# A mixture-of-experts product on one core: the last P4 pair unsplit, P3 begun with a pair

## The chip, the core and the metric

The kernel runs on one core of one Trainium2 chip. The metric is the device time of one execution in microseconds (us). In the text TensorE (PE) multiplies matrices, VectorE (DVE) and ScalarE (ACT) work on tiles and empty TensorE's accumulators, GpSimd (POOL) and SyncE (SP) mostly issue DMA transfers; ScalarE issues some too. Every engine takes its instructions in program order.

## What is computed

Each token is multiplied by all eight experts' matrices, and the results are added with softmax weights:

```python
def reference(x, router_logits, expert_weights):      # (16, 512, 512), (16, 512, 8), (8, 512, 2048)
    probs = softmax(router_logits, axis=-1)
    output = np.zeros((16, 512, 2048), np.float32)
    for e in range(8):
        output += probs[:, :, e:e+1] * np.matmul(x, expert_weights[e])
    return output
```

Put differently: with the tokens in one row of 8192 and the scaled inputs p_e * x of all experts side by side, the output is one product of an 8192 x 4096 and a 4096 x 2048 matrix.

## The kernel before

**Three levels of fast products.** The kernel forms that product with seven multiplications in place of eight, on three levels. On the outer level the tokens are cut into 16 blocks q of two halves of 256, the experts into two groups of four and the output columns into two halves; the seven outer products are called P1, P2, P5, P6, P7, P4 and P3 and run in about this order, each for all sixteen q. On the middle level an outer product of one q (class `Product`, line 566) has seven steps in the order of `STEPS` (1, 5, 6, 2, 7, 3, 4; line 353). Each step is eight matmuls of 128 x 128 by 128 x 512, for which it needs a left operand (128 tokens) and a right one, called a weight here, one for each step. On the innermost level steps 1 and 5 of a *pair* of products can be done together by seven smaller products each (`by_thirds`, line 781): 56 matmuls of half width in place of 32 of full width. A stage in which that is done is called split here.

**Stages.** `add` (line 672) puts one or two products into a stage; stages run one after another (`run`, line 849). In a pair the steps alternate: step 1 of the first product, step 1 of the second, and so on. Work beside the products is hung on a stage and a slot (`at`, line 669): slots count the steps of the stage, 0 to 13 in a pair and 0 to 6 in a single; in a split stage slots 0 to 3 are spread over the split part. k4 is the first stage of P4 and k3 the first of P3; P4 has eight pairs, k4 to k3-1, all of them split. P3 has a single (3,0) in stage k3, seven pairs in k3+1 to k3+7, and a single (3,15) in the last stage, `end` = k3+8; k3+2 to k3+7 are split. (3,0) stands for product P3 of q = 0.

**Left operands.** A `Left` (line 445) is made by VectorE out of two loads, xT and pT, in two halves (`queue_make`), with a difference d (`queue_s2`) and an interpolation (`queue_i`, z<-z,d). For P3 a third load is subtracted from each half, the left operand of P6 that was put by in DRAM (`ZBlock`, line 494, w<-z in the profile). It takes a buffer of tag w. The operands of a stage are made in the stage before it (`queue_lefts`), their loads begin two stages before (`start_loads`), unless a hook places them (`load_z`, line 1152).

**Weights.** P3's seven weights come from DRAM with one 1 MB load each, issued by ScalarE (`fetch_w`, line 162, w<-wd in the profile): three were stored as they are (tag b22), four are sums that were made in parts during P4 (`by_parts`, line 1071). `turnover` (line 1128) hangs the seven fetches, in the order of STEPS, on slots counted on from a stage, 14 to a pair. For split stages the weights of steps 1 and 5 are cut up into sums of their own (`third_sums`, line 178, called by `make_third`, line 1159), one more buffer of tag w each.

**The w buffers.** The pool `wpool` has 15 buffers of 1 MB with tag w. They hold, in P4 and P3: the seven weights of the outer product, two third sums, in each split stage a room tile for the sums of the left operands, in each split stage of P4 a keep tile (`keep_in_w`, line 1210) in which results wait that go to DRAM at the end of the stage (out_dram<-keep), the tile of `by_parts`, the seven weights of the next outer product as they come, and the ZBlocks of P3. A new tile gets the buffer that the program gave up first; the instruction that first writes it waits until the last user of the old tile is done, and what is behind it on its engine waits too.

**Order on VectorE.** A list of tasks is filled by hooks and emptied by `slack` (line 384): after each step it puts as many tasks into VectorE's program as a count of its time leaves room for. `post` (line 582) puts in what empties the accumulators: on P4, which adds to a base that was loaded from DRAM (h<-out_dram), six of seven posts are VectorE's and one (step 2, line 616) is ScalarE's; on P3 two are VectorE's and five ScalarE's. The base of the corner (1,0) is loaded by hook into a half of the keep tile (keep<-out_dram, lines 929 to 933), those of the others into h tiles. The results go out through GpSimd, where they are added to what is in DRAM.

**The end.** The last product, (3,15), adds to a base of its own, whose four parts are fetched in the stage before it (lines 1173 to 1177).

Of the kernel before, what the change touches and what calls it, by code (L numbers as in the profile page):

```python
# [31 lines left out]
def kernel(  # L32
# [84 lines left out]
    def sp(o, i):  # L117
        note(nc.sync.dma_start(out=o, in_=i))

    def pool(o, i, **how):  # L120
        note(nc.gpsimd.dma_start(out=o, in_=i, **how))  # L121
# [40 lines left out]
    def fetch_w(what, kn):  # L162
        t = new_w()
        note(nc.scalar.dma_start(out=t, in_=stored[what, kn]))  # L164
        return t
# [12 lines left out]
    def third_sums(w):  # L178

        t = new_w().rearrange("p (s c) (h n) -> p s c h n", s=2, h=2)  # L180
        t = {5: t[:, 0, :, 0], 6: t[:, 0, :, 1], 7: t[:, 1, :, 0], 4: t[:, 1, :, 1]}
        b = w.rearrange("p (k c) (h n) -> p k c h n", k=2, h=2)
        tt(t[5], b[:, 0, :, 1], b[:, 0, :, 0], SUB)
        tt(t[6], b[:, 1, :, 1], t[5], SUB)
        tt(t[7], b[:, 1, :, 1], b[:, 0, :, 1], SUB)
        tt(t[4], b[:, 1, :, 0], t[6], SUB)
        return {**t, 1: b[:, 0, :, 0], 2: b[:, 1, :, 0], 3: b[:, 1, :, 1]}
# [186 lines left out]
    def need(task):  # L374
        if task is not None and not task.done:
            flush(task)
            clock["pe"] = max(clock["pe"], clock["dve"])

    def later(cost, make, first=False):
        t = Task(cost, make)  # L380
        (queue.appendleft if first else queue.append)(t)
        return t
# [246 lines left out]
    def out_rows(q, odd, cols, tn):  # L629
        t, n = tn  # L630
        return out_f[ds((2 * q + odd) * HQ + t * HP, HP), ds(cols * NH + n * NB, NB)]

    def to_out(q, odd, cols, **how):
        return lambda tn, o: pool(out_rows(q, odd, cols, tn), o, **how)
# [22 lines left out]
    def base_of(q):  # L657
        if q % 2:
            return WideBase(out_f[ds(2 * q * HQ, HQ), ds(NH, NH)]
                            .rearrange("(t p) (n m) -> p t n m", t=2, n=2))  # L660
        return Base(lambda tn: out_rows(q, 0, 1, tn))

    INNER = ((0, 0), (1, 1), (0, 1), (1, 0))


    stages = []
    hooks, late, wait_for = {}, {}, {}

    def at(stage, slot, make):
        hooks.setdefault((stage, slot), []).append(make)  # L670

    def add(*products):
        stages.append(products)
        return len(stages) - 1
# [11 lines left out]
    def left_of(r, q, fresh=True):  # L686
        a, b = 2 * q, 2 * q + 1
        if r == 1:
            pt = PBlock(a, P1, xp1[q - 2][1] if q in (2, 3) else None)
            if q in (2, 3):  # L690
                xs[a] = XBlock(a, xp1[q - 2][0])
            return Left(xblock(a), pt), [xblock(a), pt]
        if r in (2, 4):
            h, pt = (a, PBlock(a, P2)) if r == 2 else (b, PBlock(b, P2))
            return Left(xblock(h), pt), [xblock(h), pt]
        if r == 5:
            pt = PBlock(b, PQ)
            return Left(xblock(b), pt), [xblock(b), pt]
        if r == 6:
            pt = PBlock(a, P1)  # L700
            return Left(xblock(a), pt, of=lefts[5, q]), [xblock(a), pt]
        h = a if r == 3 else b
        pt = PBlock(h, P2)
        if r == 7 and q >= 14:
            return Left(xblock(h), pt, kept=lefts[6, q]), [xblock(h), pt]
        kept_z = ZBlock(q)
        return Left(xblock(h), pt, kept=kept_z), [xblock(h), pt, kept_z]

    def kept_rows(q):
        return lambda tn: kept[q][tn[1], ds(tn[0] * HP, HP), :]  # L710

    def product(r, q, **how):
        left, loads = left_of(r, q)
        lefts[r, q] = left
        p = None
        if r == 1:
            def sink(tn, o):
                pool(kept_rows(q)(tn), o)
            p = Product(right[1], left, sink)
        elif r == 2:  # L720
            if q >= QK:
                base = products[1, q].o.__getitem__
            else:
                base = bases[2, q] = Base(kept_rows(q))
            p = Product(right[2], left, to_out(q, 0, 0), base)
        elif r == 5:
            bases[6, q] = m1 = Base(kept_rows(q))
            m1.task = {}

            p = Product(right[5], left, to_out(q, 1, 0))  # L730
        elif r == 6:
            m1 = bases[6, q]

            def base(tn):
                need(m1.task[tn])
                return m1.t[tn]
            p = Product(right[6], left, to_out(q, 0, 1), base)
        elif r == 7:
            base = bases[7, q] = base_of(q) if q < 14 else products[6, q].o.__getitem__
            p = Product(right[7], left, to_out(q, 1, 1), base)  # L740
        elif r == 4:
            base = bases[4, q] = Base(lambda tn: out_rows(q, 1, 1, tn))
            p = Product(right[4], left, to_out(q, 1, 0, accum_op=ADD), base)
        else:
            p = Product(right[3], left, to_out(q, 0, 1, accum_op=ADD), **how)
        p.loads = loads
        products[r, q] = p
        return p
# [30 lines left out]
    thirds = {}  # L779
# [91 lines left out]
    def fetch_at(stage, slot, base, *tns):  # L871
        for tn in tns:
            at(stage, slot, lambda tn=tn: base.fetch(tn))
# [8 lines left out]
    for i in range(0, QK + 1, 2):  # L882
        k = add(product(2, rest[i]), product(2, rest[i + 1]))
# [14 lines left out]
            ks.setdefault(r, add(product(r, q), product(r, q + 1)))  # L898
    k7, k4 = ks[7], ks[4]
    xs.clear()  # L900
    k3 = add(product(3, 0))
    for q in range(1, 15, 2):
        add(product(3, q), product(3, q + 1))
    end = add(product(3, 15))

    def claim(of, tn):
# [7 lines left out]
    for q in range(16):  # L914
        k = k5 + 1 + q
# [6 lines left out]
    def base_at(stage, slot, r, q, *tn):  # L922
        at(stage, slot, lambda: bases[r, q].fetch(*tn))
    for q in range(0, 14, 2):
        k = k7 + 1 + q // 2
# [3 lines left out]
    for q in range(16):  # L929
        k = k4 + q // 2  # L930
        for slot, tn in zip((6, 8, 10), INNER):
            base_at(k - 1, slot, 4, q, tn)
        base_at(k, 4, 4, q, INNER[3], lambda k=k: thirds[k].kept.pop())


    def wedge(kn, e):
# [122 lines left out]
    def slots_after(stage, slot, n):  # L1059
        slot += n  # L1060
        while slot >= 7 * len(stages[stage]):
            slot -= 7 * len(stages[stage])
            stage += 1
        return stage, slot
# [63 lines left out]
    def turnover(stage, slots, r, raw):  # L1128

        right[r].w = {}  # L1130

        def fetch(p):
            if p in RAW:
                right[r].w[p] = fetch_w(raw, RAW[p])
            else:
                right[r].w[p] = fetch_w((r, p), (0, 0))
        for slot, p in zip(slots, STEPS):
            at(*slots_after(stage, slot, 0), lambda p=p: fetch(p))
    turnover(k6 - 1, range(2, 15, 2), 7, "t3")
    turnover(k4 - 1, range(0, 13, 2), 4, "t4")  # L1140
    turnover(k3 - 2, (4, 12, 18, 19, 20, 21, 24), 3, "b22")

    for q in range(16):
        z_dram[q] = dram.tile([P, 2 * K8, HQ], f16, name=f"z_{q}")
# [3 lines left out]
        k, half_way = k5 + 1 + q, 7 * len(stages[k5 + q]) * 9 // 14  # L1148
# [3 lines left out]
    def load_z(stage, slot, r, q):  # L1152
        load = products[r, q].loads[-1]
        load.by_hook = True
        at(stage, slot, load.begin)
# [3 lines left out]
    def make_third(stage, slot, r, p):  # L1159
        def make():  # L1160
            third_of[r][p] = third_sums(right[r].w[p])
        at(stage, slot, lambda: third_made[r].append(later(2.76, make)))
# [1 line left out]
    make_third(k4 - 1, 7, 4, 1)  # L1164
    make_third(k4 - 1, 9, 4, 5)
    load_z(k3 - 2, 8, 3, 0)
    load_z(k3 - 1, 11, 3, 1)
    load_z(k3 - 1, 12, 3, 2)
    make_third(k3 - 1, 8, 3, 1)
    make_third(k3 - 1, 9, 3, 5)  # L1170


    finish = products[3, 15]
    finish.base = Base(lambda tn: out_rows(15, 0, 1, tn))
    finish.sink = lambda tn, o: sp(out_rows(15, 0, 1, tn), o)
    for slot, tn in zip((6, 8, 10, 12), INNER):
        fetch_at(end - 1, slot, finish.base, tn)
    finish.steps = (1, 5, 6, 3, 7, "2a", 4, "2b")
    cols = {"2a": ds(0, NB // 2), "2b": ds(NB // 2, NB // 2)}
# [30 lines left out]
    def keep_in_w():  # L1210
        t = wpool.tile([P, 4, NB], f32, name="keep", tag="w")
        return [t[:, i] for i in range(4)]
    for r, first, to, keep in ((4, k4, k3, keep_in_w), (3, k3 + 2, end, None)):
        for stage in range(first, to):
            thirds[stage] = Thirds(*(p.left for p in stages[stage]), third_of[r], new_w, keep, third_made[r])
    need_first = [right[1].task[p] for p in (6, 7, 4)]
# [41 lines left out]
```

## Time and profile before

| | |
|---|---|
| three runs, median (lowest to highest) | 1377.53 us (1374.09 to 1378.62) |
| profiled execution, its time | 1377.51 us |
| its span, first to last instruction | 1375.8 us |
| granted TensorE clock, mean | 0.994 |
| matmuls | 6798 |
| DMA | 388.43 MB, 282 GB/s on the mean |
| HBM | 241.21 MB read, 173.21 MB written |

The page of a profile lists, for each engine, busy time, share of the span and number of instructions; its other views used here are the list of waits (who waited for what: total us, times, longest us), the timeline (start us, duration us, engine, line, operation, out<-in, count, and in brackets the idle time before with what ended it), the chain of waits (the work that ended last, followed back; start us, duration us, what), the groups of instructions (busy us, mean ns of one, idle time before), the DMA issues (count, KB of each, median us from issue to landing) and windows (for a stretch of time: its length, each engine's busy us and number of instructions, TensorE's clock, DMA share, GB/s). A queue such as ACTq or SPq is the part of the engine that issues; a DMA on it is shown with the time that issuing took. DMA lines with GB/s cut a stretch into 40 equal slices. An engine's idle time matters only where TensorE then waits for it.

### The profile page before, as it was taken

To read this page: it belongs to the slowest core of one execution; us is meant where nothing else is said; L and a number is where in the kernel's file an instruction comes from. 1 tells how busy PE (TensorE), PEld (TensorE's weight loads), DVE (VectorE), ACT (ScalarE), POOL (GpSimd) and SP (SyncE) were. 2 spreads that over 40 slices of the span, in tenths; PEclk is the share of its full clock that TensorE was granted. 3 is DMA by queue.
4 is the path that set the end of the run, shared out by engine and by line. 5 is a ranking of instruction groups with operands and counts; after the bars stand their busy time and mean duration, and the time that the engine had idled before them with its cause. 6 is when DMAs were issued, how large, how long until landed. Compare 5 with 4: busy or idle time off the path is not lost.

```text
span 1375.8 us, 18714 instructions
## 1 busy us (share of the span) xinstructions
PE 1360.0 (99%) x6798; PEld 663.1 (48%) x6798; DVE 1120.3 (81%) x1386; ACT 228.1 (17%) x453; POOL 410.9 (30%) x652
## 2 busy tenths in 40 slices
PE   9999999999999999999999999999999999799998
PEld 4555444444444444444444444444555555256554
DVE  7877767579789888887978888988888889678884
ACT  3232111100011111111111100000111111133331
POOL 3223233331222343323332122222143423133231
PEclk9999999999999999999999999999999999799999
DMA  9998999999899999999999999998999999999976
GB/s 184 224 246 234 212 260 249 254 288 387 249 289 295 337 343 314 306 280 292 340 266 297 392 383 392 360 355 292 335 224 276 264 294 304 305 280 237 218 107 127
DMA packets 199229, 388.43 MB, mean 282 GB/s; under 512 B 53728, under 2 KB 87776, under 8 KB 191584
## 3 DMA queue, kind: packets, MB, share of 16 engines
q0 software_dynamic: 88688, 185.12, 55.4%
q1 hardware_dynamic: 106416, 173.68, 39.6%
q10 hardware_dynamic: 4032, 28.44, 5.3%
q8 instruction: 53, 0.87, 0.2%
q14 instruction: 40, 0.33, 0.1%
HBM read 241.21 MB, written 173.21 MB: 301 GB/s over the span
## 4 chain that ended last, share of the span: by engine, by line
PE 94%; DMA 4%; issue 1%; POOL 1%; ACTq 0%; ACT 0%; POOLq 0%
PE ps L130 71%; PE pt L130 23%; DMA w<-wd 2%; DMA out_dram<-keep 1%; DMA w<-in_expert_weights_dram 1%; POOL out_dram L121 0%; ACTq L164 0%; POOL w L121 0%; ACT h L616 0%; ACT h L1202 0%; POOL ident L225 0%; POOLq L121 0%; ACTq L616 0%; POOLq L225 0%; POOLq L1242 0%
## 5 line engine op out<-in xcount | busy, mean ns | idle before, releaser
L130 PE MATMUL ps<-w,z 128*128 128x512 f16 (+1 forms) x3760 | 823.6, 376 | 7.2 <-DMA w<-wd 7.2
L130 PEld LDWEIGHTS <-z 128*128 128x128 f16 x5280 | 517.6, 98 | 595.9 <-issue 14.8
L121 POOL DMA_DIRECT2D out_dram<-h x336 | 217.6, 664 | 681.7 <-ACT h L616 312.9
L130 PE MATMUL pt<-w,z 128*128 128x512 f16 (+1 forms) x1520 | 324.7, 361 | 2.4 <-DMA w<-wd 2.2
L107 DVE TENSOR_TENSOR h<-ps,h 128x512 f32<-128x512 f32 x253 | 171.6, 687 | 126.3 <-PE ps L130 114.1
L107 DVE TENSOR_TENSOR z<-xT,pT 128x2048 f16<-128x2048 f16 x220 | 266.3, 1217 | 3.9 <-DMA xT<-xs 2.8
L130 PE MATMUL ps<-w,d 128*128 128x512 f16 x880 | 199.2, 379 | 0.0
L130 PEld LDWEIGHTS <-d 128*128 128x128 f16 x880 | 86.1, 98 | 100.2
L107 DVE TENSOR_TENSOR z<-z,d 128x2048 f16<-128x2048 f16 x110 | 132.2, 1217 | 0.0
L107 DVE TENSOR_TENSOR w<-w 128x1024 f16<-128x1024 f16 (+2 forms) x116 | 116.3, 1016 | 2.4 <-PE ps L130 1.0
L603 ACT COPY h<-ps 128x512 f32<-128x512 f32 x90 | 52.8, 587 | 376.4 <-PE ps L130 366.6
L107 DVE TENSOR_TENSOR h<-pt,h 128x512 f32<-128x512 f32 x111 | 76.1, 687 | 42.0 <-PE pt L130 36.8
L616 ACT COPY h<-ps 128x512 f32<-128x512 f32 x57 | 33.4, 587 | 363.9 <-PE ps L130 337.2
L107 DVE TENSOR_TENSOR d<-z 128x1024 f16<-128x1024 f16 x110 | 74.5, 684 | 0.8
L107 DVE TENSOR_TENSOR z<-z,w 128x2048 f16<-128x2048 f16 x60 | 73.5, 1225 | 2.0
L107 DVE TENSOR_TENSOR ps<-ps,h 128x512 f32<-128x512 f32 (+1 forms) x77 | 48.3, 629 | 20.4 <-PE ps L130 15.9
L121 POOL DMA_DIRECT2D wd<-w x86 | 47.3, 550 | 53.9 <-DVE w L107 17.8
L121 POOL DMA_DIRECT2D w<-in_expert_weights_dram x65 | 49.0, 791 | 38.7 <-DMA wd<-w 28.2
L130 PEld LDWEIGHTS <-w 128*128 128x128 f16 x528 | 48.7, 98 | 8.1 <-DMA w<-in_x_dram 1.6
L121 POOL DMA_DIRECT2D kept<-h x56 | 30.8, 550 | 67.2 <-ACT h L603 35.1
L599 ACT COPY h<-ps 128x512 f32<-128x512 f32 x63 | 35.4, 600 | 74.9 <-PE ps L130 72.0
L107 DVE TENSOR_TENSOR h<-h 128x512 f32<-128x512 f32 (+2 forms) x69 | 45.2, 675 | 0.1
(81 smaller groups left out, 455.3 us busy)
## 6 DMA issues: line engine op xcount, KB each, us to landing
out_dram<-h POOLq DMA_DIRECT2D x336, 256.0 KB, 7.8
w<-z SPq DMA_DIRECT2D x30, 1024.0 KB, 12.6
pT<-p_dram SPq DMA_DIRECT2D x108, 256.0 KB, 9.6
w<-wd ACTq DMA_DIRECT2D x27, 1024.0 KB, 10.2
h<-kept SPq DMA_DIRECT2D x100, 256.0 KB, 7.2
h<-out_dram SPq DMA_DIRECT2D x80, 256.0 KB, 13.9
wd<-w POOLq DMA_DIRECT2D x72, 256.0 KB, 8.5
xT<-x SPq DMA_DIRECT2D x71, 256.0 KB, 10.3
```

What stands on the lines that cost most here:

```text
L107: dve(nc.vector.tensor_tensor(out=o, in0=a, in1=b, op=op))
L121: note(nc.gpsimd.dma_start(out=o, in_=i, **how))
L130: note(nc.tensor.matmul(ps, z, w, start=start, stop=stop, skip_group_check=True))
L599: act(nc.scalar.copy(o[tn], q if p == 5 else x))
L603: act(nc.scalar.copy(o[TN[p]], b if p == 2 else x))
L616: act(nc.scalar.copy(o[tn], b))
```

## The change

The order of P3's products and what hangs on it:

- the last P4 pair, stage k3-1, is no longer split, has no keep tile and no room tile, and its two (1,0) bases go into h tiles at slot 3;
- P3 consists of seven pairs, k3 to k3+6, then the single (3,14) in k3+7, then the single (3,15) as before. Split are k3+1 to k3+6;
- P3's weights 1, 5, 6, 2, 7, 3, 4 are fetched in k3-3 at slots 4 and 12, in k3-2 at slots 6 and 10, and in k3-1 at slots 2, 4 and 6. Before, they were fetched in k3-2 at slots 4 and 12 and in k3-1 at slots 4, 5, 6, 7 and 10;
- the ZBlocks of (3,0) and (3,1) come in k3-2 at slots 8 and 12, those of (3,2) and (3,3) at the first two slots of k3; before, that of (3,0) came in k3-2 at slot 8, those of (3,1) and (3,2) in k3-1 at slots 11 and 12;
- the third sums of P3's weights are queued at the start of k3 and no longer in k3-1;
- the bases of (3,15) are fetched at slots 1 to 4 of the stage before it, now a single, in place of slots 6, 8, 10 and 12 of a pair.

```diff
     k7, k4 = ks[7], ks[4]
     xs.clear()
-    k3 = add(product(3, 0))
-    for q in range(1, 15, 2):
+    k3 = len(stages)
+    for q in range(0, 14, 2):
         add(product(3, q), product(3, q + 1))
+    add(product(3, 14))
     end = add(product(3, 15))
...
             base_at(k - 1, slot, 4, q, tn)
-        base_at(k, 4, 4, q, INNER[3], lambda k=k: thirds[k].kept.pop())
+        if k < k3 - 1:
+            base_at(k, 4, 4, q, INNER[3], lambda k=k: thirds[k].kept.pop())
+        else:
+            base_at(k, 3, 4, q, INNER[3])
...
-    turnover(k3 - 2, (4, 12, 18, 19, 20, 21, 24), 3, "b22")
+    turnover(k3 - 3, (4, 12, 20, 24, 30, 32, 34), 3, "b22")
...
     load_z(k3 - 2, 8, 3, 0)
-    load_z(k3 - 1, 11, 3, 1)
-    load_z(k3 - 1, 12, 3, 2)
-    make_third(k3 - 1, 8, 3, 1)
-    make_third(k3 - 1, 9, 3, 5)
+    load_z(k3 - 2, 12, 3, 1)
+    load_z(k3, 0, 3, 2)
+    load_z(k3, 1, 3, 3)
+    make_third(k3, 0, 3, 1)
+    make_third(k3, 0, 3, 5)
...
-    for slot, tn in zip((6, 8, 10, 12), INNER):
+    for slot, tn in zip((1, 2, 3, 4), INNER):
         fetch_at(end - 1, slot, finish.base, tn)
...
-    for r, first, to, keep in ((4, k4, k3, keep_in_w), (3, k3 + 2, end, None)):
+    for r, first, to, keep in ((4, k4, k3 - 1, keep_in_w), (3, k3 + 1, end - 1, None)):
         for stage in range(first, to):
             thirds[stage] = Thirds(*(p.left for p in stages[stage]), third_of[r], new_w, keep, third_made[r])
```

## The prediction

> **What bounds the kernel now.** I read the first part of the page, then the list of waits, then the timeline of TensorE around the only place where it waits for long. The profiled execution took 1377.51 us, of which 1375.8 us are the span; the median of the three runs shown is 1377.53 us, so the sum below, made against the profiled execution, stands for the median too.
>
> ```profile
> PE 1360.0 (99%) x6798; PEld 663.1 (48%) x6798; DVE 1120.3 (81%) x1386; ACT 228.1 (17%) x453; POOL 410.9 (30%) x652
> PE ps L130 <- DMA w<-wd: 7.2, 3, 4.6
> PE pt L130 <- DMA w<-wd: 2.2, 1, 2.2
> ```
>
> TensorE sets the time. All that it waits for after the start is 9.4 us in four waits for weights (w<-wd), and the timeline of TensorE puts them side by side, in the single product (3,0) with which P3 begins (stage k3):
>
> ```profile
> 1169.39 1.89 PE L130 MATMUL pt<-w,z 128*128 128x512 f16 x8
> ...
> 1174.24 1.90 PE L130 MATMUL ps<-w,z 128*128 128x512 f16 x8 [1.23 <-DMA w<-wd]
> 1180.75 3.57 PE L130 MATMUL ps<-w,z 128*128 128x512 f16 x8 [4.62 <-DMA w<-wd]
> 1186.48 3.57 PE L130 MATMUL pt<-w,z 128*128 128x512 f16 x8 [2.16 <-DMA w<-wd]
> 1191.37 7.54 PE L130 MATMUL ps<-w,z 128*128 128x512 f16 x24 [1.32 <-DMA w<-wd]
> 1198.75 3.62 PE L130 MATMUL pt<-w,z 128*128 128x512 f16 x16
> ...
> 1219.47 1.04 PE L130 MATMUL pt<-w,z 128*128 128x256 f16 x8
> ...
> 1242.85 1.04 PE L130 MATMUL pt<-w,z 128*128 128x256 f16 x8
> ```
>
> A step is eight matmuls. From 1198.75 to 1219.47 twelve unhindered steps pass: 1.727 us each. From 1169.39 (step 5 of the single) to 1198.75 (step 5 of the next pair) there are eight steps, 13.8 us, but 29.36 us go by: 15.5 us are lost. That is more than the 9.4 us of waiting, since eight matmuls take 3.57 us instead of 1.89 after the longest wait. The chain of waits, the timeline of ScalarE and its queue, and that of GpSimd tell why the weights are late:
>
> ```profile
> 1145.47 14.28 DMA out_dram<-keep
> ...
> 1162.57 28.75 DMA w<-wd
> ```
>
> ```profile
> 1134.12 0.59 ACT L616 COPY h<-ps 128x512 f32<-128x512 f32 x1 [1.14 <-PE ps L130]
> 1139.56 0.33 ACTq L164 DMA_DIRECT2D w<-wd  x1
> ...
> 1159.81 1.63 ACTq L164 DMA_DIRECT2D w<-wd  x3
> 1161.56 0.59 ACT L616 COPY h<-ps 128x512 f32<-128x512 f32 x1 [10.61 <-DVE z L107]
> ```
>
> ```profile
> 1122.16 0.86 POOL L121 DMA_DIRECT2D out_dram<-keep  x1 [0.46 <-DVE keep L107]
> ```
>
> Five of P3's seven weights are asked for in the last P4 stage, k3-1. The first of them waits until the keep tile of stage k3-2 has been written out (1145.47 + 14.28 = 1159.75), and then five fetches go out within 3 us; the last lands at 1191.33 (1162.57 + 28.75). The fifteen buffers of tag w are handed on in the order in which the program gives them up: the third tiles and the room tile of k3-1, idle once the split part ends, 23.38 - 10 x 1.727 = 6.1 us into the stage, go to later requests. The second fetch, too, goes out at 1139.56, 4.9 us after ScalarE's copy has ended: it takes the keep tile of k3-3, whose last write was issued at 1122.16.
>
> **The change, part by part.**
>
> *One split less.* A split stage lasts 1242.85 - 1219.47 = 23.38 us, an unsplit pair 14 x 1.727 = 24.18 us. P4 has seven split stages for eight; P3 keeps six. Cost +0.80 us, on the path.
>
> *Weights earlier.* The seven fetches move from k3-2 (two) and k3-1 (five) to k3-3 (two), k3-2 (two) and k3-1 (three). The unsplit k3-1 needs no room tile and no keep tile, and the two third tiles of P4 come free one stage earlier, at about 1127. Handing the buffers on in order: weight 1 takes the keep tile of k3-5, weight 5 that of k3-4, weight 6 the tile of the last part sums, weight 2 a third tile, weight 7 the other one. All of these are free before they are asked for or soon after, so weights 1, 5, 6, 2 and 7 land tens of us before k3 begins at 1144.28 + 24.18 = 1168.46 (the single began one step before 1169.39, at 1167.66, and k3-1 and k3-2 each 23.38 us earlier, at 1144.28 and 1120.90). Weights 3 and 4 get the first weight of P4 and the keep tile of k3-2, free at 1159.75; in a pair each step lasts 3.45 us, so weight 3 is needed at 1168.5 + 5 x 3.45 = 1185.7. ScalarE may stand until 1160 with the two copies of step 2 (due at 1156.4 and 1158) behind it. The same happens now without cost: the copy of k3-1 runs at 1161.56 after 10.61 us, and TensorE does not wait. Gain: the whole 15.5 us; 1377.5 - 15.5 + 0.8 = 1362.8 us if nothing else is late.
>
> *What is late next: the left operand of (3,0).* Its load (call it z0, w<-z) keeps its slot in k3-2, but the buffer that it gets is now the keep tile of k3-3, which weight 5 had. That is not free before about 1139.5, as the fetch above shows, where z0 went out at 1129.77 before:
>
> ```profile
> 1129.77 0.33 SPq L118 DMA_DIRECT2D w<-z  x1
> 1131.78 4.49 SPq L118 DMA_DIRECT2D h<-out_dram  x2
> w<-z SPq DMA_DIRECT2D x1, 1024.0 KB, 20.7
> w<-z SPq DMA_DIRECT2D x2, 1024.0 KB, 11.4
> w<-z SPq DMA_DIRECT2D x3, 1024.0 KB, 13.9
> 1144.48 0.69 DVE L107 TENSOR_TENSOR keep<-ps,keep 128x512 f32<-128x512 f32 x1 [0.44 <-PE ps L130]
> 1157.66 1.23 DVE L107 TENSOR_TENSOR z<-z,w 128x2048 f16<-128x2048 f16 x1
> L107 DVE TENSOR_TENSOR z<-z,d 128x2048 f16<-128x2048 f16 x110 | 132.2, 1217 | 0.0
> L107 DVE TENSOR_TENSOR d<-z 128x1024 f16<-128x1024 f16 x110 | 74.5, 684 | 0.8
> ```
>
> Behind it on SP stand two bases h of k3-1, then the load z1 of (3,1), xT and pT. z0 lands 11.4 to 20.7 us after its issue (the DMA issues of the three stages k3-2, k3-1, k3), so between 1150.9 and 1160.2. VectorE comes to it sooner than the 1157.66 of before: without the third sums and the sums for a split k3-1 its queue is empty at the end of k3-2, and after its last addition at 1145.2 stand one interpolation (1.22), the first post (0.69), the other one (1.22), the second post (0.69) and the product of the operand (1.22): it waits for z0 from 1150.2. Behind that wait stand the posts of steps 5 and 6. The second post of step 6 comes 1.22 + 2 x 0.69 + 0.69 + 0.69 + 2.45 + 0.69 = 7.1 us after z0 has landed, and TensorE needs it for its tenth step at 1144.28 + 9 x 1.727 = 1159.8. So what z0 lands later than 1152.7 is lost. Ends: nothing, and 7.5 us, to which slow matmuls add up to 2 x 1.68 (3.57 - 1.89). From the middle duration, 13.9, and 1.5 us more for the keep tile, whose write now runs beside two fetches more, z0 lands at 1154.9: I take 2.5 us with the base loads behind it. Whether the clock falls in so short a gap decides another 1.7 us; after 1.23 us in the rows above it did not (1.90), after 4.62 it did, so I take none.
>
> The Trainium skill, TensorE: Matmul & The Clock Gate, Part 1, puts the fall at an idle window of about 3.4 us. By that rule a wait of 2.5 us keeps the full clock, and the trace, with 1.23 and 4.62 us on its two sides, agrees.
>
> *Third sums.* Moved from k3-1 into k3: four subtractions each, two times.
>
> ```profile
> 1163.72 2.61 DVE L107 TENSOR_TENSOR w<-w 128x1024 f16<-128x1024 f16 x4
> L107 DVE TENSOR_TENSOR z<-xT,pT 128x2048 f16<-128x2048 f16 x220 | 266.3, 1217 | 3.9 <-DMA xT<-xs 2.8
> ```
>
> Before k3+1 can start, VectorE has in k3: two interpolations 2.4, third sums 5.2, two operands 4.9, the sums of the split 2.8, four posts 2.8: 18.1 of 24.2 us. z2 and z3, asked for at the start of k3 or up to 10 us earlier when SP gets there, are used 8.8 us into k3 at the earliest; with 13.9 us to land they are late by at most 5 us, within the 6.1 that VectorE has over. Cost 0; without that cover 5.
>
> *The two (1,0) bases of k3-1* come into h tiles at step 3 in place of the keep tile: the same two 256 KB loads, used in its last steps some 17 us later. Cost 0.
>
> *Single (3,14) next to last.* The four bases of the last product are fetched in steps 1 to 4 of a single stage of 12.1 us; they land in 3.2 us and are used a stage later. VectorE needs in that stage four halves of the operand (4.9), d (0.7), one interpolation (1.2) and two posts (1.4), 8.2 of 12.1 us. Cost 0; without cover at most those 3.2 us. After the last matmul nothing changes.
>
> ```profile
> h<-out_dram SPq DMA_DIRECT2D x3, 256.0 KB, 3.2
> ```
>
> Sum: 1377.5 - 15.5 + 0.8 + 2.5 = 1365.3 us.
>
> **The rivals.**
>
> *z0 is the new wait.* With 20.7 us to land it comes at 1160.2: 7.5 us lost and 1 to 2 us of slow clock, about 1372. For it: the 20.7 of the same stage. Against: that load followed four bases and stood beside a fetch; the next five took 11.4 and 13.9.
>
> *DMA has no room.* Here are the stages k3-3 to k3+1:
>
> ```profile
> 1097.50:1120.90 23.40, 23.40 (x137) 13.31 (x136) 20.09 (x31) 4.10 (x10) 9.13 (x13) 1.00 1.08 284
> 1120.90:1144.30 23.40, 23.40 (x138) 13.31 (x137) 20.20 (x29) 4.09 (x10) 7.40 (x9) 1.00 1.08 298
> 1144.30:1167.70 23.40, 23.40 (x138) 13.34 (x137) 21.77 (x29) 4.09 (x10) 6.01 (x8) 1.00 0.97 306
> 1167.70:1193.10 25.40, 16.08 (x54) 5.73 (x53) 13.34 (x15) 2.33 (x4) 4.76 (x6) 0.72 1.04 312
> 1193.10:1219.30 26.20, 26.20 (x117) 11.60 (x116) 20.00 (x23) 5.83 (x10) 5.17 (x6) 0.95 1.07 315
> GB/s 378 326 322 312 350 266 280 280 273 252 263 266 252 245 224 235 294 333 319 336 357 364 326 193 161 144 175 172 224 252 378 420 434 434 378 434 420 434 357 368
> ```
>
> These 121.8 us move 36.9 MB (last column times length). The new order does the same up to the first split P3 stage, less one product (a z, xT, pT and four outputs, 2.6 MB), in 2 x 23.4 + 2 x 24.2 = 95.1 us: 361 GB/s. At the 315 GB/s of the last row 34.3 MB take 108.9 us, 13.8 more: 1376.6 us, no change. For it: a DMA share of 1.0 in every row. Against: the slices of k3-1 (last line) reach 434 GB/s once weights are under way, and writes may trail into the next stages.
>
> The Trainium skill, HBM Reference, Specifications (TRN2), gives about 358 GB/s as a core's share and some 425 for a core alone. By the share the 34.3 MB would take 95.8 us, 0.7 too long; the slices above exceed it.
>
> *Slower: the fetch of weight 5 stops ScalarE before a split.* It now stands in k3-3 and takes the keep tile of k3-4. The copies of k3-2's split part are behind it on ScalarE, and TensorE's banks wait for those:
>
> ```profile
> 1098.74 0.86 POOL L121 DMA_DIRECT2D out_dram<-keep  x1 [0.22 <-issue]
> 1121.59 0.79 ACT L818 COPY ps<-pt 128x256 f32<-128x256 f32 x2 [10.26 <-PE pt L130]
> out_dram<-keep POOLq DMA_DIRECT2D x3, 256.0 KB, 16.7
> out_dram<-keep POOLq DMA_DIRECT2D x2, 256.0 KB, 29.9
> ```
>
> It decides from the point where the write takes over 1121.6 - 1098.7 = 22.9 us: 16.7 in k3-2, but 29.9 in k3 under five fetches. At 29.9 us the copies are 7 us late, the keep tile of k3-3 follows (z0 not before 1159 + 13.9 = 1173, 13 us more), with 2 to 4 us of slow clock: 1362.8 + 7 + 13 + 2 = 1385. Against: only one fetch runs beside that write.
>
> **How the numbers follow.** Forecast (0 to 5 us of new waiting, 1362.8 to 1368) 0.56, at 1365.3; z0 as the new wait, about 1372 (1369 to 1374), 0.20; no room for DMA, about 1376.6, 0.12; slower, about 1385, 0.12. A measurement of this kernel can tell about 0.3%, 4.1 us, from no change: below 1373.4 is faster, above 1381.7 slower. Faster takes the forecast and nearly all of the second: 0.75; the same 0.14; slower 0.11. The range begins 1.3 us below a change without any new wait, since the runs of before lie up to 3.4 us under their median, and ends at 1375, which leaves out the slower case and most of the DMA case.
>
> **What would show it.** Right: no wait of TensorE for w<-wd in k3; P4's last stage 24.2 us plus a gap of 1 to 4 us about its ninth or tenth step, with VectorE waiting for w<-z at about 1150 until 1153 to 1157; the w<-z issue at 1139 to 1143; five fetches issued before 1140; k3+1 starting at once. Wrong: waits for w<-wd in k3 as now, a late L818 copy in k3-2, or a gap at the start of k3+1 behind third sums or z2.

## The result, and the profile after

The changed kernel takes 1382.88 us (median of six runs, 1381.00 to 1384.23) against 1377.00 us of the kernel before in the same session: a ratio of 1.0043 (95% interval 1.0029 to 1.0056). It is slower by 0.4%, where 1365.3 us and "faster" were forecast. The profiled execution, the longest of the six, has a span of 1382.5 us, 6.7 us longer than before.

The list of TensorE's waits, after:

```profile
PE ps L130 <- DVE h L107: 16.8, 2, 9.2
```

The four waits for weights are gone. Two waits for VectorE stand in their place. The timeline of TensorE shows where:

```profile
1148.09 3.62 PE L130 MATMUL pt<-w,z 128*128 128x512 f16 x16
1151.54 3.62 PE L130 MATMUL ps<-w,d 128*128 128x512 f16 x16
1154.99 3.62 PE L130 MATMUL ps<-w,z 128*128 128x512 f16 x16
1166.20 6.07 PE L130 MATMUL ps<-w,z 128*128 128x512 f16 x16 [7.59 <-DVE h L107]
1172.10 3.62 PE L130 MATMUL pt<-w,z 128*128 128x512 f16 x16
...
1182.46 3.62 PE L130 MATMUL pt<-w,z 128*128 128x512 f16 x16
...
1196.28 3.62 PE L130 MATMUL pt<-w,z 128*128 128x512 f16 x16
1209.12 5.10 PE L130 MATMUL ps<-w,z 128*128 128x512 f16 x16 [9.22 <-DVE h L107]
1214.05 1.05 PE L130 MATMUL pt<-w,z 128*128 128x256 f16 x8
```

In a pair the first row with pt<-w,z x16 is step 5 of both products, the second one step 3. In k3 these are 1196.28 - 1182.46 = 13.82 us apart, undisturbed. In k3-1 they are 1172.10 - 1148.09 = 24.01 apart: **gap 1** costs 10.2 us (7.59 of waiting, the rest in sixteen matmuls that took 6.07 us instead of 3.62). From step 3 of k3 to the first split matmul of k3+1, 6.9 us where nothing is late (read in the last experiment below), pass 1214.05 - 1196.28 = 17.77: **gap 2** costs 10.9 us. Together 21.1. The span of before, less 15.5, plus 0.8 and 21.1, gives 1382.2 us; 1382.5 was measured, so nothing else of size has moved.

The timelines of VectorE and ScalarE, and of SP's queue:

```profile
1162.52 1.22 DVE L107 TENSOR_TENSOR z<-z,w 128x2048 f16<-128x2048 f16 x1 [10.88 <-DMA w<-z]
...
1204.46 1.23 DVE L107 TENSOR_TENSOR z<-z,w 128x2048 f16<-128x2048 f16 x1 [13.69 <-DMA w<-z]
```

```profile
1118.01 0.33 ACTq L164 DMA_DIRECT2D w<-wd  x1
1118.51 1.08 ACT L616 COPY h<-ps 128x512 f32<-128x512 f32 x2 [13.96 <-DVE h L107]
1119.75 0.33 ACTq L164 DMA_DIRECT2D w<-wd  x1
```

```profile
1147.13 0.33 SPq L118 DMA_DIRECT2D w<-z  x1
...
1172.71 0.33 SPq L118 DMA_DIRECT2D w<-z  x1
...
1181.81 5.12 SPq L118 DMA_DIRECT2D w<-z  x2
```

Both gaps are VectorE waiting for a load w<-z: z0 for gap 1 (issued at 1147.13, used at 1162.52), z3 for gap 2 (the second of the two issued from 1181.81 on, at 1186.61). The chain of waits leads from one to the other:

```profile
1123.23 23.84 DMA out_dram<-keep
...
1147.61 24.86 DMA out_dram<-keep
...
1173.09 13.45 DMA w<-wd
...
1186.61 17.76 DMA w<-z
...
1204.46 1.24 DVE z L107
```

The write of the keep tile of k3-3 takes 23.84 us (17.33 before), and z0 has its buffer. The write of the keep tile of k3-2 takes 24.86 us (14.28 before) and lands at 1172.47; weight 3 has that buffer and goes out at 1172.64; weight 4 stands behind it on ScalarE's queue and goes out at 1173.09; and z3 goes out when weight 4 has landed.

Why should an operand wait for a weight of another queue? In this program the transfers that SP and ScalarE issue share eight completion counters in turn: each waits until the one eight before it, in the order of both queues together, has landed. The trace shows it here: z5, the load before z3, went out at 1181.81, when weight 3 had landed (1172.64 + 9.10 = 1181.74), and z3 at 1186.61, when weight 4 had (1173.09 + 13.45 = 1186.54). z3 got the counter of weight 4. The two loads of the pair after next, with z4 and z5, stand ahead of z3 on SP, because `run` calls `start_loads` at the end of slot 0, and the hook of z3 hangs on slot 1.

The windows of k3-3, k3-2, k3-1 and 24 us behind them, to be compared with those of before (last three columns: clock, DMA share, GB/s):

```profile
1097.90:1121.30 23.40, 23.40 (x138) 13.32 (x137) 20.08 (x31) 4.00 (x10) 6.75 (x12) 1.00 1.05 292
1121.30:1144.60 23.30, 23.30 (x137) 13.26 (x136) 20.01 (x27) 4.10 (x10) 10.31 (x12) 1.00 1.07 289
1144.60:1168.50 23.90, 16.31 (x71) 7.11 (x70) 11.42 (x14) 0.00 (x0) 1.72 (x2) 0.84 1.07 321
1168.50:1192.60 24.10, 24.10 (x106) 10.58 (x105) 20.50 (x26) 5.15 (x9) 7.50 (x9) 0.94 0.93 297
```

Before, the four rows had 284, 298, 306 and 312 GB/s. More is asked for earlier, but hardly more is moved.

### The profile page after: what moved, and what is told of

It is laid out like the page before. It is cut to its first block, busy times and chain, and to the rows that moved or that the text cites. A ratio compares the mean times of both kernels' runs of the same rounds, so it can differ in the third digit from the quotient of the medians.

```text
span 1382.5 us, 18640 instructions
## 1 busy us (share of the span) xinstructions
PE 1360.0 (98%) x6774; PEld 661.3 (48%) x6774; DVE 1115.7 (81%) x1378; ACT 225.3 (16%) x445; POOL 411.8 (30%) x652
## 4 chain that ended last, share of the span: by engine, by line
PE 91%; DMA 7%; issue 1%; DVE 0%; POOL 0%; ACTq 0%; ACT 0%; POOLq 0%; DVEq 0%; SPq 0%
PE ps L130 68%; PE pt L130 23%; DMA out_dram<-keep 4%; DMA w<-z 1%; DMA out_dram<-h 1%; DMA w<-wd 1%; DMA w<-in_expert_weights_dram 1%; POOL out_dram L121 0%; DVE w L107 0%; POOL w L121 0%; DVE z L107 0%; DVE keep L107 0%; DVE h L107 0%; ACTq L164 0%; ACT h L1207 0%
## 5 line engine op out<-in xcount | busy, mean ns | idle before, releaser
L130 PE MATMUL pt<-w,z 128*128 128x512 f16 (+1 forms) x1536 | 328.1, 361 | 0.4 <-DMA w<-in_expert_weights_dram 0.4
L107 DVE TENSOR_TENSOR ps<-ps,h 128x512 f32<-128x512 f32 (+1 forms) x77 | 48.3, 629 | 18.8 <-PE ps L130 17.5
L121 POOL DMA_DIRECT2D kept<-h x56 | 30.9, 551 | 71.4 <-ACT h L603 39.3
```

Of the source, the lines that this page charges most:

```text
L107: dve(nc.vector.tensor_tensor(out=o, in0=a, in1=b, op=op))
L130: note(nc.tensor.matmul(ps, z, w, start=start, stop=stop, skip_group_check=True))
```

## The experiments

The expectations name four theories for gap 1. A: ScalarE stands before the fetch of weight 1 (the copies of step 2, at 1109.02 and 1110.74 before, run at 1118.51), GpSimd's outputs are held up behind those copies, and the keep tile behind the outputs. B: the DMA engines have no room for the weights' bytes beside P4's own traffic. C: there is room, and only what is asked for first must be what is needed first. D: it is the number of transfers, through the eight counters. Gap 2 is put down to the place of z3 on SP. All ratios are to the kernel before, with 95% intervals; edits are made to the changed kernel.

**z3 one slot earlier.**

```diff
-    load_z(k3, 1, 3, 3)
+    load_z(k3, 0, 3, 3)
```

> The changed kernel with one edit: the load of (3,3)'s left operand, z3, stands at slot 0 of k3 instead of slot 1, so ahead of the loads of stage k3+2 on SP. Theory A (order of the queue): z3 was late (issued at 1186.6, landed at 1204.4) because it stood behind z5 and behind two weight fetches; now it goes out beside z2 at about 1173 and lands by 1187, the wait of 13.7 us on VectorE and the gap of 9.2 us on TensorE at the end of k3 go, the one of 7.6 us in k3-1 stays: about 10 to 11 us less than the changed kernel, ratio to before 0.995 to 0.998. Theory B (DMA has no room in these stages): z3 lands after 1195 all the same, the second gap stays over 4 us, ratio 1.001 or more.

1371.39 us, 0.9957 (0.9942 to 0.9972). TensorE's timeline has one gap left, and the chain of waits before it is that of gap 1:

```profile
1164.94 6.04 PE L130 MATMUL ps<-w,z 128*128 128x512 f16 x16 [6.21 <-DVE h L107]
```

```profile
1122.63 21.91 DMA out_dram<-keep
...
1144.60 16.57 DMA w<-z
```

z3 is issued at 1170.10, 16.5 us sooner, and lands at 1183.66. Gap 2 is gone, 11.5 us of the median with it: one slot decides the sign of the whole change, as theory A of that run had it (order of the queue). Gap 1 stays: 22.62 us from step 5 to step 3 of k3-1, 8.8 lost. The runs below that have z3 first show gap 1 alone.

**Weight 1 fetched after ScalarE's copies.**

```diff
-    turnover(k3 - 3, (4, 12, 20, 24, 30, 32, 34), 3, "b22")
+    turnover(k3 - 3, (8, 12, 20, 24, 30, 32, 34), 3, "b22")
```

> The changed kernel with one edit: P3's weight 1 is fetched in k3-3 at slot 8, after ScalarE's two copies of step 2, instead of slot 4, ahead of them; weight 5 stays at slot 12. The same bytes leave at about the same time. Theory A: the copies run at 1109 to 1111 (1118.5 in the changed kernel), the keep tile of k3-3 lands at about 1140 instead of 1147, z0 goes out 7 us earlier, the gap in k3-1 falls from 7.6 us to 0 to 3 us, the second gap stays: ratio to before 0.996 to 1.000. Theory B: the two fetches crowd the writes out wherever they stand on ScalarE; keep lands after 1145, the gap stays over 5 us, ratio 1.003 to 1.005.

1383.79 us, 1.0048 (1.0033 to 1.0063). ScalarE's timeline shows the copies on time and TensorE's shows the gap no smaller:

```profile
1109.22 0.59 ACT L616 COPY h<-ps 128x512 f32<-128x512 f32 x1 [4.82 <-PE ps L130]
1110.95 0.59 ACT L616 COPY h<-ps 128x512 f32<-128x512 f32 x1 [1.14 <-PE ps L130]
1115.83 2.66 ACTq L164 DMA_DIRECT2D w<-wd  x2
```

```profile
1168.57 5.60 PE L130 MATMUL ps<-w,z 128*128 128x512 f16 x16 [8.60 <-DVE h L107]
```

The keep tile of k3-3 is written at 1145.63, 1.4 us sooner than in the changed kernel. The held-up copies were real and cost next to nothing: theory A, which expected the tile at about 1140, falls.

**z0 in another buffer.** Weight 2 is fetched two slots earlier and takes the keep tile's buffer; z0 gets a third tile, free long before.

```diff
-    turnover(k3 - 3, (4, 12, 20, 24, 30, 32, 34), 3, "b22")
+    turnover(k3 - 3, (4, 12, 20, 22, 30, 32, 34), 3, "b22")
-    load_z(k3 - 2, 8, 3, 0)
+    load_z(k3 - 2, 9, 3, 0)
```

> The changed kernel with one edit: z0 is asked for at slot 9 of k3-2 (before: slot 8) and weight 2 at slot 8 (before: 10), so weight 2 gets the buffer of the keep tile of k3-3 and z0 that of a third tile, idle since 1127. The late copies and the bunched writes of k3-3 stay as they are. Theory A (z0 is late because of its buffer): z0 goes out at 1136 to 1141, lands by 1155, first gap 0 to 3 us; the second stays; ratio 0.996 to 1.000. Theory B: z0 still lands after 1160 as transfers are slow, gap over 5 us, ratio 1.003 or more.

1380.99 us, 1.0027 (1.0015 to 1.0040). From the timelines of TensorE and the chain of waits:

```profile
1163.57 6.00 PE L130 MATMUL ps<-w,z 128*128 128x512 f16 x16 [5.11 <-DVE h L107]
```

```profile
1139.40 20.39 DMA w<-z
```

z0 goes out 7.7 us sooner, as the forecast had it, but takes 20.39 us instead of 15.30. Two thirds of what the buffer gave were taken back by the transfer itself, and gap 1 still costs 1169.40 - 1147.93 - 13.82 = 7.65 us. The ratio lies between what theory A (up to 1.000) and theory B (1.003 or more) expected.

**Weights 1 and 5 through GpSimd's queue.**

```diff
-        note(nc.scalar.dma_start(out=t, in_=stored[what, kn]))
+        if by is None:
+            note(nc.scalar.dma_start(out=t, in_=stored[what, kn]))
+        else:
+            by(t, stored[what, kn])
...
+            by = pool if r == 3 and p in (1, 5) else None
...
```

> The changed kernel with one edit: weights 1 and 5 are fetched at the same slots of k3-3 by GpSimd's queue instead of ScalarE's. Same bytes, same stage, no fetch ahead of ScalarE's copies. Theory A: copies of k3-3 at 1109 to 1111, writes spread as before the change, z0 out at about 1140, first gap 0 to 3 us, second gap stays; ratio 0.996 to 1.000. Theory B: as the bytes are the same, the gap stays over 5 us, ratio 1.003 to 1.005.

1380.86 us, 1.0024 (1.0013 to 1.0035). The two fetches have left the counters of SP and ScalarE, and still the write of the keep tile lands at 1145.97, only 1.1 us sooner. So those counters alone do not hold it; but GpSimd, which now issues the fetches too, starts the write at 1126.88 instead of 1123.23, and the write takes 19.09 us, less than 23.84 and more than the 17.33 of before. z0 goes out at 1146.03 and lands after 12.95 us; TensorE waits 3.96 and 0.68 us in gap 1, which still costs 6.2 us, and 9.62 in gap 2. The ratio again lies between the two forecasts.

**z0 before the weights.** z3 in slot 0; weight 1 is fetched late (slot 22), and z0 has its place in k3-3.

```diff
-    turnover(k3 - 3, (4, 12, 20, 24, 30, 32, 34), 3, "b22")
+    turnover(k3 - 3, (22, 12, 20, 24, 30, 32, 34), 3, "b22")
-    load_z(k3 - 2, 8, 3, 0)
+    load_z(k3 - 3, 4, 3, 0)
-    load_z(k3, 1, 3, 3)
+    load_z(k3, 0, 3, 3)
```

> z3 at slot 0 of k3 (as in the run before that removed the second gap) and, in addition, z0 and weight 1 change places: z0 is loaded in k3-3 at slot 4 by SP, weight 1 is fetched in k3-2 at slot 8 by ScalarE. The same megabytes leave in each stage. Theory C (z0 is late because it is asked for after weights that are needed 18 us later than it): z0 lands by 1140, the first gap goes, time 8 to 10 us under the run with z3 alone, 1361 to 1364 us, ratio 0.988 to 0.990. Theory B in its strong form (no room for these bytes in k3-3 and k3-2 in any order): the gap moves to another transfer, the bases of k3-2 or z1, with 4 us or more; ratio 0.993 or more.

1372.10 us, 0.9969 (0.9958 to 0.9981): no better than with z3 alone. z0 is there at 1116.7, and VectorE's timeline has other waits instead, in front of a gap of 5.55 us:

```profile
1154.40 0.69 DVE L107 TENSOR_TENSOR h<-pt,h 128x512 f32<-128x512 f32 x1 [1.40 <-DMA h<-out_dram]
1158.86 0.69 DVE L107 TENSOR_TENSOR h<-pt,h 128x512 f32<-128x512 f32 x1 [3.76 <-DMA h<-out_dram]
1163.33 0.69 DVE L107 TENSOR_TENSOR h<-ps,h 128x512 f32<-128x512 f32 x1 [3.18 <-DMA h<-out_dram]
```

The bases of k3-1 now take 17 to 21 us to land, with z3 alone 14 to 20. Theory C, in which the order alone was wrong, expected the gap to go.

**All weights later, with z3 first and without.** The fetches start in k3-2 and k3-1.

```diff
-    turnover(k3 - 3, (4, 12, 20, 24, 30, 32, 34), 3, "b22")
+    turnover(k3 - 3, (24, 26, 28, 30, 36, 37, 38), 3, "b22")
```

> z3 at slot 0 of k3, and no fetch in k3-3: weights 1 and 5 in k3-2 at slots 10 and 12, 6 and 2 in k3-1 at slots 0 and 2, 7, 3 and 4 in k3-1 at slots 8, 9 and 10. z0 stays in k3-2 at slot 8, and its buffer is then one that is long free. Theory B (the two fetches of k3-3 slow the writes and z0): the keep tile of k3-3 lands at about 1139, z0 goes out at about 1130 and lands by 1151, no gap in k3-1; the weights come by 1168 to 1185 as they are needed; ratio 0.988 to 0.990. If the first gap has another cause (the order on VectorE alone), it stays at 5 us or more, 0.995. If the later fetches come too late, TensorE waits for w<-wd in k3.

> As the run before, with z3 left at slot 1 of k3 (behind the loads of stage k3+2): the later weights alone. Theory A for the second gap (z3 behind z5, which waits for weights 3 and 4): the first gap goes and the second stays or grows, since weights 3 and 4 land later here: ratio 0.996 to 1.000. If the second gap were a consequence of the first (all that is late in k3-1 makes k3 late), both would go: 0.988 to 0.990.

With z3 first: 1378.62 us, 1.0004 (0.9979 to 1.0030), but single runs lie between 1366.55 and 1381.47, so this order has no settled time; why is open. The 0.988 to 0.990 of theory B did not come, though the keep tile was written at 1136.94, as it expected. In the profiled execution z0 took 22.0 and z1 30.9 us to land, and TensorE has five waits of 0.35 to 6.19 us between k3-1 and the end of k3. Without: 1390.00 us, 1.0107 (1.0083 to 1.0131), slower than either forecast; the profiled execution, at 1382.89, was the fastest of five. There z0 goes early and gap 1 is gone, and TensorE's timeline has this alone:

```profile
1206.96 5.94 PE L130 MATMUL ps<-w,z 128*128 128x512 f16 x16 [16.79 <-DVE h L107]
```

Gap 2 grows from 9.22 to 16.79 us though nothing is late before it. It belongs to z3's place behind weight 4, not to gap 1: z3 lands at 1202.21 here and landed at 1204.36 in the changed kernel, and TensorE, which comes to k3 9.7 us sooner, waits for it all the longer.

**Twice as many transfers, the same bytes.** z3 first; weights 1, 5, 6 and 2 in two transfers of 512 KB each.

```diff
-        note(nc.scalar.dma_start(out=t, in_=stored[what, kn]))
+        for i in range(parts):
+            c = ds(i * K8 // parts, K8 // parts)
+            note(nc.scalar.dma_start(out=t[:, c], in_=stored[what, kn][:, c]))
...
+            parts = 2 if r == 3 and p in (1, 5, 6, 2) else 1
...
```

> z3 at slot 0, and weights 1, 5, 6 and 2 fetched in two transfers of 512 KB each instead of one of 1 MB: four transfers more, not a byte more. Theory D (SP and ScalarE together have eight transfers under way; each waits until the one eight before it has landed, so the number of transfers counts): the transfers behind them are held up further, z0 or the bases of k3-1 go out and land later, the gap in k3-1 grows from 6.2 us to 8 us or more; ratio 0.997 or more. Theory B (bytes alone): the gap stays at 5 to 7 us; ratio 0.994 to 0.997 as with z3 alone.

1370.73 us, 0.9952 (0.9935 to 0.9968), against 1371.39 with whole fetches: no difference that can be told. TensorE's timeline still has a gap:

```profile
1161.66 3.37 PE L130 MATMUL ps<-w,z 128*128 128x512 f16 x8 [2.79 <-DVE h L107]
```

With three shorter waits after it, 7.3 us are lost between step 5 of k3-1 and step 5 of k3, 8.8 with whole fetches. Four more transfers through the eight counters made nothing worse, so theory D in its plain form, a price for each transfer, falls.

**Weights behind the bases.** z3 first; z0 in k3-3, then the bases of k3-1, then the weights.

```diff
-    turnover(k3 - 3, (4, 12, 20, 24, 30, 32, 34), 3, "b22")
+    turnover(k3 - 3, (22, 24, 26, 28, 30, 32, 34), 3, "b22")
-    load_z(k3 - 2, 8, 3, 0)
+    load_z(k3 - 3, 4, 3, 0)
...
```

> z3 at slot 0, z0 in k3-3 at slot 4, and all weights behind the six bases of k3-1: in k3-2 at slots 8, 10 and 12, in k3-1 at slots 0, 2, 4 and 6, in the order of use. Ahead of the bases stands one transfer more than before the change (z0), where the run with z0 in weight 1's place had three. Theory D: the bases go out by 1138 and land by 1156 as before the change, z0 is long there, the gap in k3-1 is 0 to 2 us, weights land by 1175; 1362 to 1366 us, ratio 0.988 to 0.992. Theory B: the same bytes leave within 20 us less, something else of k3-1 lands late; gap over 4 us, ratio 0.995 or more.

1371.92 us, 0.9968 (0.9956 to 0.9980). The bases are out by 1137.76, as the order meant, and take 16 to 28 us, the last until 1165.97; weights 1, 5 and 6, issued behind them on ScalarE's queue at 1139.8 to 1143.8, take 8.7 to 14.3. VectorE's timeline:

```profile
1157.18 0.69 DVE L107 TENSOR_TENSOR h<-pt,h 128x512 f32<-128x512 f32 x1 [3.75 <-DMA h<-out_dram]
1161.64 0.69 DVE L107 TENSOR_TENSOR h<-ps,h 128x512 f32<-128x512 f32 x1 [3.17 <-DMA h<-out_dram]
```

Asking first did not help: the weights overtake what was asked for before them. Theory C falls.

**Two parts at once, then three.** z3 first, weights 1 and 5 by GpSimd, z0 in the other buffer (the edits above together):

> z3 at slot 0, weights 1 and 5 fetched by GpSimd at their slots in k3-3, z0 in the third tile's buffer (slot 9, weight 2 at slot 8): two transfers fewer in SP's and ScalarE's eight, and no wait for the keep tile. Theory D with the buffer: z0 goes out at about 1136 and lands by 1153, gap 0 to 2 us; ratio 0.988 to 0.992. Theory B: z0 takes about 20 us as in the two runs with one of these edits, gap 4 us or more; ratio 0.994 or more.

1369.99 us, 0.9948 (0.9933 to 0.9963), the lowest median of the kernels that compute all of the product, but not told apart from z3 alone. z0 takes 16.7 us to land. TensorE's timeline has a shorter gap 1, which costs 4.1 us:

```profile
1162.89 5.30 PE L130 MATMUL ps<-w,z 128*128 128x512 f16 x16 [2.26 <-DVE h L107]
```

With the halved fetches as well:

> z3 first, weights 1 and 5 by GpSimd, z0 in the other buffer, and weights 1, 5, 6 and 2 in two transfers of 512 KB each: no bytes less than with z3 first. Theory B: the same bytes have to move in the same stages; the wait can be spread, not removed: 1368 to 1371 us, 2 to 5 us lost in k3-1. If the order alone were the cause, the parts would add up (1370.0 with two of them, 1370.7 with the third): 1364 to 1367 us.

1372.71 us, 0.9964 (0.9947 to 0.9981). The parts do not add up, as B expected and an order to be mended did not; the forecast of B itself, 1368 to 1371, was a little low. Four waits of 0.45 to 1.71 us stand where one of 6.21 stood with z3 alone: the wait is spread, not removed, and five more, of 0.30 to 1.10 us for ScalarE, follow between 1211 and 1230.

**Half the bytes.** z3 first; of weights 1, 5, 6 and 2 only the first half is fetched and used twice.

```diff
...
-        note(nc.scalar.dma_start(out=t, in_=stored[what, kn]))
-        return t
+        c = ds(0, C if cut else K8)
+        note(nc.scalar.dma_start(out=t[:, c], in_=stored[what, kn][:, c]))
+        return HalfW(t) if cut else t
...
+            cut = r == 3 and p in (1, 5, 6, 2)
...
```

> The third sums' load z3 before the loads of the next pair, and weights 1, 5, 6 and 2 of P3 are fetched in their first half only (512 KB instead of 1 MB each); the first half is used twice in the products, so P3's result differs, and the matmuls and additions are as many as before. So there are as many transfers as with z3 first alone (1371.4 us, gap 1 of 6.2 us in k3-1), and 2 MB less. Theory B (bytes: the weights take the room of the other transfers): 2 MB at some 315 GB/s are 6.7 us, so z0 lands before 1157 and gap 1 shrinks to 0 to 2 us: 1363 to 1367 us. Theory D (the number of transfers, each waiting for the one eight before it): the number is the same, the gap stays over 4 us: 1369 to 1372 us.

1365.83 us, 0.9923 (0.9909 to 0.9936), in the middle of what B expected. Timeline of TensorE and chain of waits:

```profile
1147.89 3.62 PE L130 MATMUL pt<-w,z 128*128 128x512 f16 x16
...
1160.24 1.89 PE L130 MATMUL ps<-w,z 128*128 128x512 f16 x8 [1.82 <-DVE h L107]
1163.23 1.89 PE L130 MATMUL ps<-w,z 128*128 128x512 f16 x8 [1.10 <-DVE h L107]
1164.95 3.62 PE L130 MATMUL pt<-w,z 128*128 128x512 f16 x16
...
1189.13 3.62 PE L130 MATMUL pt<-w,z 128*128 128x512 f16 x16
...
1196.03 1.04 PE L130 MATMUL pt<-w,z 128*128 128x256 f16 x8
```

```profile
1122.32 17.37 DMA out_dram<-keep
...
1139.74 16.73 DMA w<-z
```

Same places, same number of transfers, 2 MB less: the write of the keep tile takes 17.37 us as before the change, not 21.91, and gap 1 costs 1164.95 - 1147.89 - 13.82 = 3.2 us, not 8.8. The bytes of the weights make most of gap 1: 5.6 of 8.8 us go with half of them, a little less than B expected. Smaller fetches also give their counters back sooner, but that is not what let z0 go: in both kernels it went out when the keep tile had been written (1144.54 and 1139.69; z0 at 1144.60 and 1139.74), and the transfer that had its counter before had landed some 4 us earlier, at 1140.38 and 1135.96. The write itself was issued 0.3 us sooner and took 4.5 us less. What the counters did to the other loads beside it is not told apart. The last two rows of TensorE give the undisturbed 6.9 us used above.

## Why the prediction was wrong

*Weights earlier: right.* The 15.5 us came back whole: no wait for w<-wd is left in k3. The buffers were handed on as worked out: weight 5 took the keep tile of k3-4, z0 that of k3-3, weight 3 that of k3-2. But of the five fetches expected before 1140 only three had gone out: those of weights 2 and 7 went at 1147.87 and 1151.87, each when a base that had its counter had landed (1147.85 and 1151.85). The forecast looked at buffers alone and not at the counters; for these two fetches that cost nothing, for z3 it did.

*One split less, +0.8; bases (1,0) and the end at no cost: right.* The balance of the spans closes to 0.3 us with these.

*z0, "I take 2.5 us": right in mechanism, wrong in size; 10.2 us.* VectorE came to z0 at about 1151.6 (forecast 1150.2). "What z0 lands later than 1152.7 is lost" held in three kernels: landings at 1162.43, 1161.17 and 1156.47 give 9.7, 8.5 and 3.8; measured were 10.2, 8.8 and 3.2. That it fits so well is partly luck: in the first two 2.4 us of the loss are slow matmuls, which the rule leaves out, and the waiting was some 2 us less than it says. What failed is "1.5 us more for the keep tile, whose write now runs beside two fetches more": the write took 6.5 us more, the write's issue came 1.1 us later, and z0 left at 1147.13 in place of 1139.5 + 1.5; its own 15.3 us were near the 13.9 taken. With half the bytes the keep tile was free at 1139.69. So the rival "DMA has no room" was the mechanism of this gap, for 10.2 us rather than 13.8, and the forecast had priced it into z0 with 1.5. The rival had the bytes right: from the start of k3-3 to the first split P3 stage 34.32 MB moved, in 116.2 us at 295 GB/s; with z3 in slot 0 it was 306 GB/s on the mean, far from the 361 that the forecast needed.

*Third sums, "z2 and z3, asked for at the start of k3 or up to 10 us earlier ... Cost 0": the step that failed.* z3 was asked for 7.6 us after the start of k3 (1186.61; k3 begins two steps, 3.45 us, before 1182.46) and landed after 17.8 us instead of 13.9. The forecast took it that SP would get to z3 with z2; it did not follow SP's order, in which a hook in slot 1 stands behind xT, pT and z of the next pair but one. And it looked only at z3's own duration, not at what its issue waits for: a weight, whose buffer waits for a keep tile's write. Cost 10.9 us. With gap 2 removed the kernel is faster than before by 0.43%, at 1371.39 us, near the rival "z0 is the new wait" (about 1372), though z0 was late by its issue and not by the 20.7 us to land that this rival took. With gap 1 removed and z3 left in its place (all weights later) nothing was won: gap 2 then costs 1212.74 - 1186.55 - 6.9 = 19.3 us. The sign was lost here.

*ScalarE behind the fetches.* It stood until 1172.47 and not until 1160 (its copies ran at 1173.60), and no wait of TensorE for it followed from that. The rival in which weight 5 stops ScalarE before a split did not come: that keep write took 17.5 us, below its 22.9. ScalarE was stopped one fetch earlier, by a base load whose counter weight 1 had (landed at 1117.91, the fetch went out at 1118.01), and the run with the copies on time shows no price for it.

*The clock.* The forecast kept the full clock for a wait of 2.5 us. After 2.26 us it fell: sixteen matmuls took 5.30 instead of 3.62 us; after 1.82 us it did not.

## What to carry to other kernels

When a fetch is moved earlier, price it by what the transfers beside it lose, not by whether its buffer is free: in a stage whose DMA share is 1 already, earlier bytes make something else late, and reordering chooses only what. For each load that a hook places, read what stands ahead of it in its queue's program order and what its issue waits for, counters and recycled buffers included. Check this first where a change looks free: one slot of one hook was worth 11 us here, where moving whole transfers about in the earlier stages gained 2 us at most.

## What was not expected of the hardware

Transfers issued early do not land early when another queue is busy. While the last writes of the keep tiles of k3-3 and k3-2 (256 KB, GpSimd's queue) went from 17 and 14 to 24 and 25 us, and in k3-2 the loads on SP (256 KB) took 14 to 18 (15 to 21 before), the five 1 MB fetches on ScalarE's queue in k3-3 to k3-1 landed in 7.8 to 10.8 us. The Trainium skill, DMA: Bandwidth & Descriptors, Queues, rings and completion order, says that each DMA engine takes turns between the queues that have work for it, a packet at a time. By that rule a queue with a single transfer gets as many turns as one with eight. The trace agrees for ScalarE's and SP's: in the 9.02 us of the fetch issued at 1130.64 ScalarE's queue, with this one transfer, had 27.6% of the DMA engines' time and moved 1.05 MB; SP's, with six or seven transfers under way, had 26.8% and moved 0.80 MB. GpSimd's, with the outputs, had 51.4% for 0.85 MB. On GpSimd's queue, among those outputs, the fetches of weights 1 and 5 took 16.0 and 18.3 us.

The clock fell after idle times of 2.26 and 2.79 us and not after 1.82 us. The rule that the prediction weighed (the Trainium skill, TensorE: Matmul & The Clock Gate, Part 1: about 3.4 us) is too long for these two; the same section says that its window runs freely and that its effect varies from run to run with the phase. The granted clock of these runs shows the grid: within a run it changes only at times that are whole multiples of 3.41 us apart, and then lies at 0.50 for 3.41, 6.83, 10.24 or 17.07 us. In the run with GpSimd's queue the wait of 3.96 us fell on two such stretches: the one with 1.87 us of idle time in it left the clock high, the one with 2.09 brought it down. The measurement decides: an idle time of over 2 us is to be priced with some 1.7 us of slow clock in this kernel.
